# The one-hot of the first layer's expert slots: four comparisons instead of one, and its products two product groups later

## The chip, the cores and the metric

The kernel runs on one core of a Trainium2 chip. The metric is the device time of one execution in microseconds (us). TensorE is called PE here, its weight load PEld, VectorE DVE, ScalarE ACT, GpSimd POOL and SyncE SP, as in the profile.

## The reference, cut to what matters

Two layers of a network over 256 latent and 256 context tokens of width 1024. Each layer ends in a mixture of 16 experts of which every token uses two. The first layer sends all 512 tokens through it, and that is the part that the change touches:

```python
combine = jnp.sum(jax.nn.one_hot(expert_idx, N_EXPERTS, dtype=jnp.float32) * wts[..., None], axis=1)

def expert(acc, p):
    wg, wu, wd, gate_col = p
    y = (jax.nn.silu(t @ wg) * (t @ wu)) @ wd
    return acc + gate_col[:, None] * y, None
```

wg and wu are 1024 x 512, wd is 512 x 1024, all float32. The kernel does not multiply every token by every expert: for each expert it finds the tokens that chose it, gives each a slot (96 slots for an expert), gathers their rows, and multiplies only those.

## The kernel before, in words

`moe` (L1637) is called once, for the first layer, with nt = 4 tiles of 128 tokens. The second layer has functions of its own.

**Slots.** For expert e the tile `rv` holds, for each token, its rank among the tokens of that expert (0 where it did not choose it). `which` (L1678) writes the one-hot `oneh`: 128 partitions (tokens) x 4 tiles x 96 slots, 1 where the rank equals the slot's number (`iot` holds 1 to 96 in every partition). It is one DVE instruction over 384 elements, L1679. `slots_of` (L1681) multiplies the one-hot with four columns for each token (four small matmuls on PE, "products" below, into a `tr` tile of PSUM), and three small DVE instructions (L1688 to L1690) turn the sums into two index columns and a weight. `gather` (L1693) then fetches the 96 rows with an indirect DMA that POOL issues.

**The product groups.** The main loop takes the experts in order. Each expert has twelve pieces of weights: four for the gate, four for up, and four for the down product of the expert before it. They are called g0 to g3, u0 to u3 and d0 to d3 below. `gemm3` (L1751) does one piece at a time: it takes the next prepared piece, issues six matmuls of 512 columns (a product group), and calls `step`, which lets every running generator do its next bit. So whatever a generator does after its k-th `yield` is issued, on every engine, k product groups after it was begun.

**Preparing a piece.** Each piece is split into a rounded part (ACT copy, L469) and a rest (subtraction, L470), 128 x 1024 each. There are four buffers (`wb`, `wb`, `uo`, `um`), so a piece is prepared as soon as the group four before it has been multiplied. The subtraction runs on DVE for three pieces of four, and on POOL for the fourth (g3, u3, d3, all in `um`). A subtraction is called a share below.

**The generators of one expert.** `stage_a(e+3)` finds the slots and gathers: it is begun after u3 of expert e and issues the one-hot at once. After d0 it does nothing (first `yield` passed), after d1 it issues the products, after d2 the three small DVE instructions, after d3 the gather. `stage_b` (L1737) transposes gathered rows during u1 to u3. `stage_d` (L1770) issues the gating (`sg`, L1776 on DVE) after d0 and its transposes (L1781) after g1 of the next expert. `evac` scales the output rows, and `scatter` writes them back after g2.

The order on every queue is the order in which this Python program issues, and each engine takes its queue in order. The one-hots of experts 0 and 1 are made before the loop (L1826), those of experts 2 to 15 by `stage_a`, the last of them during expert 12.

Of the kernel before, what the change touches and what calls it, by code (L numbers as in the profile page):

```python
# [11 lines left out]
ALU = mybir.AluOpType  # L12
# [11 lines left out]
def bc(ap, shape):  # L24
    return ap.to_broadcast(shape)
# [64 lines left out]
def build(tc, I, out):  # L90
# [4 lines left out]
    PE, DV, SC, GP, SY = nc.tensor, nc.vector, nc.scalar, nc.gpsimd, nc.sync  # L95
# [470 lines left out]
    def quarter(u, i):  # L566

        return u[i // 4][:, 512 * (i % 4):512 * (i % 4) + 512]
# [632 lines left out]
    oh, ol = ([quarter(uo, 8 * j + c) for c in range(8)] for j in range(2))  # L1201
# [336 lines left out]
    iot = const.tile([128, 96], F32, name="iot")  # L1538
# [98 lines left out]
    def moe(l, X, streams, mem, beside, then):  # L1637
# [3 lines left out]
        nt = len(streams)  # L1641
        T = 128 * nt
        CAP = 96
# [5 lines left out]
        def mt(name, shape, bufs=1, dt=F32):  # L1649
            return mp.tile(list(shape), dt, name=name, tag=name, bufs=bufs)  # L1650
# [19 lines left out]
        def slots(rank, col):  # L1670

            oh = mt("oneh", [128, nt, CAP], dt=F32R)
            which(oh, rank)
            yield
            yield
            yield from slots_of(oh, col)

        def which(oh, rank):  # L1678
            DV.tensor_tensor(oh, bc(iot[:, None, 0:CAP], [128, nt, CAP]), bc(rank, [128, nt, CAP]), op=ALU.is_equal)  # L1679

        def slots_of(oh, col):  # L1681
            p = ps_tr()
            for t in range(nt):
                mm(p[0:CAP, 0:4], oh[:, t], col[:, t], t == 0, t == nt - 1)
            yield
            ir, ig = mt("ir", [CAP, 1], 6, I32), mt("ig", [CAP, 1], 4, I32)
            ws = mt("ws", [CAP, 1], 6)
            DV.tensor_scalar(ig, p[0:CAP, 0:1], BIG, None, op0=ALU.add)  # L1688
            DV.tensor_scalar(ir, p[0:CAP, 3:4], BIG, None, op0=ALU.add)
            DV.tensor_reduce(ws, p[0:CAP, 1:3], axis=AX.X, op=ALU.add)  # L1690
            yield ir, ig, ws
# [27 lines left out]
        def stage_a(e):  # L1719

            for r in slots(rv[:, :, 0:1, e].bitcast(F32), rv[:, :, 1:5, e]):
                if r is None:
                    yield
            ir, ig, ws = r
            IR[e] = (ir, ws)
            yield
            gather(xg[e % 2], ig)
            yield
# [38 lines left out]
        def sgt():  # L1767
            return mt("sg", [128, 512])
# [55 lines left out]
        oh = [sgt()[:, 0:nt * CAP].rearrange("p (t l) -> p t l", t=nt), mt("oneh", [128, nt, CAP], dt=F32R)]  # L1824
        for e in range(2):
            which(oh[e], rv[:, :, 0:1, e].bitcast(F32))  # L1826
# [44 lines left out]
        with tc.If(most > CAP):  # L1871
            rvD = dram.tile([128, nt * 5, 16], F32, name=f"rvD{l}")
            SY.dma_start(rvD[:, :, :], rv.bitcast(F32).rearrange("p t i e -> p (t i) e"))
            with tc.For_i(0, NEXP, 1) as e:
# [11 lines left out]
                for b in range(1, NB):  # L1886
                    DV.tensor_scalar(col[:, :, 0], col[:, :, 0], -float(CAP), None, op0=ALU.add)
                    *_, (ir, ig, ws) = slots(col[:, :, 0:1], colr)
                    gather(xg[0], ig)
                    xT = mem["ow"][2][:, 0:8 * CAP].rearrange("p (k l) -> p k l", k=8)  # L1890
# [609 lines left out]
    T, CAP = 256, 64  # L2500
# [6 lines left out]
    def pair_tile():  # L2507
        return mt("oneh", [128, 2, 2, 2, CAP], 2, F32R)
# [198 lines left out]
    with tc.If(most > CAP):  # L2707
# [3 lines left out]
        with tc.For_i(0, NEXP, 1) as e:  # L2711
# [10 lines left out]
            for b in range(1, T // CAP):  # L2722
                DV.tensor_scalar(col[:, :, 0], col[:, :, 0], -float(CAP), None, op0=ALU.add)
                oh = pair_tile()
# [68 lines left out]
```

## Time and profile before

| | us |
|---|---|
| median of 3 runs | 1588.27 (1587.4 to 1590.36) |
| the profiled execution | 1591.26 |
| its span, first to last instruction | 1589.5 |
| mean granted TensorE clock, share of full | 0.951 |
| PE busy / DVE busy / POOL busy in the span | 1397.3 / 915.4 / 617.6 |

The span is what the trace covers; the 1.76 us around it are in the time but not in the trace. The experts of the first layer run from about 650 to 965 us of the span.

### The profile page before, as it was taken

What the parts mean: (1) busy time and instruction counts of PE and PEld (TensorE: products, weight loads), DVE (VectorE), ACT (ScalarE), POOL (GpSimd) and SP (SyncE); (2) the same over time, 40 slices, a digit from 0 to 9 for tenths busy, and PEclk for the clock granted to TensorE, in tenths of its full rate; (3) what the DMA queues carried; (4) which work ended last, traced back from release to release, by engine and by line L of the source; (5) the groups of instructions that cost most, each with busy time, mean ns of one, the idle gap of its engine ahead of it and who ended that gap; (6) DMA issues with size and microseconds to landing.
All of it is one profiled execution on the core that took longest, in us unless ns stands there. A gap on an engine that the chain in (4) does not pass through costs nothing. (4 is left out here: it accounts for less than half of the span.)

```text
span 1589.5 us, 19404 instructions
## 1 busy us (share of the span) xinstructions
PE 1397.3 (88%) x7312; PEld 941.9 (59%) x7312; DVE 915.4 (58%) x1206; ACT 756.5 (48%) x1269; POOL 617.6 (39%) x398
## 2 busy tenths in 40 slices
PE   5999989877789987699999895799999888999996
PEld 2677755554466665466666673578777666444542
DVE  2665541779686466688888785635555655222223
ACT  4453435445435444477777684644444453211212
POOL 4333324877556274255555653333233223000000
PEclk8999999989899999799999998799999999999998
DMA  9266445546424153799998965422212568899994
GB/s 330 82 156 151 122 107 185 177 168 211 147 67 159 54 212 136 266 323 352 350 344 311 314 235 194 169 81 82 76 54 80 178 246 317 313 395 393 394 393 177
DMA packets 181687, 337.68 MB, mean 212 GB/s; under 512 B 7513, under 2 KB 44641, under 8 KB 181072
## 3 DMA queue, kind: packets, MB, share of 16 engines
q1 hardware_dynamic: 176112, 323.69, 59.2%
q0 software_dynamic: 4208, 8.90, 1.9%
q10 hardware_dynamic: 1264, 3.73, 0.6%
q8 instruction: 62, 1.02, 0.3%
q14 instruction: 41, 0.34, 0.1%
HBM read 329.12 MB, written 11.37 MB: 214 GB/s over the span
## 5 line engine op out<-in xcount | busy, mean ns | idle before, releaser
L470 POOL TENSOR_TENSOR wb<-wring,wb 128x1024 fp32r<-128x1024 f32 x68 | 169.6, 2497 | 276.6 <-ACT wb L469 233.6
L99 PE MATMUL acc<-hh,wb 128*128 128x512 f32 x640 | 207.4, 401 | 4.9 <-POOL wb L470 2.3
L99 PEld LDWEIGHTS acc<-hh,wb 128*128 128x128 f32 x640 | 119.7, 189 | 39.1 <-issue 5.9
L469 ACT ACTIVATE wb<-wring 128x1024 fp32r<-128x1024 f32 x88 | 92.6, 1058 | 101.8 <-PE acc L99 53.1
L99 PE MATMUL acc<-hl,wb 128*128 128x512 f32 x320 | 127.6, 399 | 0.3 <-DVE hl L595 0.2
L99 PE MATMUL acc<-wb,um 128*96 128x512 f32 (+1 forms) x480 | 120.2, 400 | 3.0 <-DVE otmp L1510 2.5
L712 DVE SCALAR_TENSOR_TENSOR ca<-u,pcol,ca 128x572 f32<-128x572 f32 x87 | 109.5, 1317 | 0.0
L99 PEld LDWEIGHTS acc<-wb,um 128*96 128x96 f32 (+1 forms) x480 | 80.4, 169 | 35.5 <-DVE otmp L1510 3.6
L2754 POOL TENSOR_TENSOR xl<-xl,fg 128x512 f32<-128x512 f32 x1 | 1.3, 1268 | 243.3 <-ACT xl L2753 243.3
L99 PE MATMUL y<-hu,hu 128*64 128x512 f32 (+2 forms) x296 | 85.4, 521 | 2.9 <-DVE hu L2137 2.8
L2586 DVE TENSOR_TENSOR sg<-sg,y 64x512 f32<-64x512 f32 x16 | 11.1, 691 | 120.6 <-ACT sg L2585 120.6
L99 PE MATMUL acc<-um,um 128*96 128x512 f32 (+2 forms) x272 | 68.1, 390 | 2.7 <-POOL um L470 2.7
L470 DVE TENSOR_TENSOR wb<-uo,wb 128x1024 fp32r<-128x1024 f32 x34 | 55.5, 1664 | 25.0 <-ACT wb L469 24.9
L99 PEld LDWEIGHTS acc<-hl,wb 128*128 128x128 f32 x320 | 60.7, 190 | 15.5 <-DVE hl L595 1.6
L470 POOL TENSOR_TENSOR um<-uo,um 128x1024 fp32r<-128x1024 f32 x19 | 48.3, 2544 | 38.9 <-ACT um L469 38.9
L99 PE MATMUL acc<-uo,um 128*96 128x512 f32 (+1 forms) x240 | 63.0, 401 | 0.0
L470 DVE TENSOR_TENSOR wb<-um,wb 128x1024 fp32r<-128x1024 f32 x30 | 51.0, 1736 | 18.3 <-ACT wb L469 18.3
L864 DVE SCALAR_TENSOR_TENSOR xa<-xin,pcol,xa 128x514 f32<-128x514 f32 x64 | 58.8, 919 | 2.3
L99 PE MATMUL acc<-wring,sT 128*32 128x512 f32 x336 | 47.9, 651 | 10.7 <-DMA wring<-in_mod_w_dram 7.6
L2585 ACT ACTIVATE sg<-y 64x512 f32<-64x512 f32 x16 | 9.5, 591 | 96.9 <-PE y L99 96.9
L99 PEld LDWEIGHTS y<-hu,hu 128*64 128x64 f32 (+2 forms) x296 | 31.8, 151 | 38.1 <-issue 33.7
L99 PEld LDWEIGHTS acc<-um,um 128*96 128x96 f32 (+1 forms) x272 | 43.5, 174 | 17.9 <-POOL um L470 3.8
(661 smaller groups left out, 3479.0 us busy)
## 6 DMA issues: line engine op xcount, KB each, us to landing
wring<-in_mod_w_dram SPq DMA_DIRECT2D x42, 1024.0 KB, 5.3
wring<-in_moe_w_gate_dram SPq DMA_DIRECT2D x18, 1024.0 KB, 7.5
uo<-in_moe_w_up_dram SPq DMA_DIRECT2D x17, 1024.0 KB, 8.1
hu<-in_moe_w_gate_dram SPq DMA_DIRECT2D x16, 1024.0 KB, 14.6
wring<-in_moe_w_down_dram SPq DMA_DIRECT2D x14, 1024.0 KB, 7.5
uo<-in_moe_w_down_dram SPq DMA_DIRECT2D x13, 1024.0 KB, 7.4
um<-in_moe_w_up_dram SPq DMA_DIRECT2D x13, 1024.0 KB, 8.0
wring<-in_hg_w_in_dram SPq DMA_DIRECT2D x13, 1024.0 KB, 5.1
```

The costliest lines, as they stand in the source:

```text
L99: PE.matmul(o, l, r, start=start, stop=stop, skip_group_check=True)
L469: SC.activation(hv, w, AF.Copy)
L470: eng.tensor_tensor(lv, w, hv.bitcast(F32), op=ALU.subtract)
L712: DV.scalar_tensor_tensor(a, x, w, a, op0=ALU.mult, op1=ALU.add)
L864: DV.scalar_tensor_tensor(a[:, 0:514], x[:, k:k + 514], par("sc_w", 16 * k + i), a[:, 0:514], op0=ALU.mult, op1=ALU.add)
L2585: SC.activation(s_[up], acc[0:CAP], AF.Silu)
L2586: DV.tensor_tensor(s_[up], s_[up], acc[up], op=ALU.mult)
L2754: GP.tensor_tensor(o, o, fg[hf], op=ALU.mult)
```

## The change

`which` writes the one-hot in four instructions, one for each tile of 128 tokens: 96 slot numbers are compared with one value per partition (that token's rank), instead of two tensors of 384 elements with each other. It concerns all 16 experts. And `slots`, from which `stage_a` takes its steps, yields four times instead of twice between the one-hot and the products. The products are thus issued after d3 instead of after d1, the three small DVE instructions after g0 of the next expert instead of after d2, and the gather after g1 instead of after d3. (The loop for experts with more than 96 tokens also calls `slots`, but takes all its steps at once.)

```diff
             oh = mt("oneh", [128, nt, CAP], dt=F32R)
             which(oh, rank)
-            yield
-            yield
+            for _ in range(4):
+                yield
             yield from slots_of(oh, col)
 
         def which(oh, rank):
-            DV.tensor_tensor(oh, bc(iot[:, None, 0:CAP], [128, nt, CAP]), bc(rank, [128, nt, CAP]), op=ALU.is_equal)
+            for t in range(nt):
+                DV.tensor_scalar(oh[:, t], iot[:, 0:CAP], rank[:, t], None, op0=ALU.is_equal)
```

## Rows read from the trace of the kernel before

**Rows 1.** The page: the chain that ended last, share of the span by engine.

```profile
PE 28%; DVE 5%; issue 2%; ACT 2%; POOL 1%; DMA 0%; POOLq 0%; DVEq 0%; ACTq 0%; SPq 0%
```

**Rows 2.** Waits of PE, 648 to 925 us (us in total, times, longest).

```profile
PE tr L99 <- DVE oneh L1679: 17.7, 11, 2.2
```

**Rows 3.** The tile `oneh`: its DVE instruction (duration ns min/median/max).

```profile
L1679 DVE TENSOR_TENSOR oneh<-iot,sm x15: 542/2273/2481, 642.1 to 904.2; 128x384 fp32r<-128x384 f32 x15
```

**Rows 4.** Timeline of one expert (start us, us, what; idle before in brackets).

```profile
759.05 2.94 PE L99 MATMUL y<-wb,um 128*96 128x512 f32 x12
...
760.45 2.43 POOL L470 TENSOR_TENSOR um<-uo,um 128x1024 fp32r<-128x1024 f32 x1 [3.64 <-ACT um L469]
...
761.02 2.27 DVE L1679 TENSOR_TENSOR oneh<-iot,sm 128x384 fp32r<-128x384 f32 x1
...
763.22 0.67 DVE L1776 TENSOR_TENSOR sg<-sg,acc 96x512 f32<-96x512 f32 x1
...
763.44 0.47 PE L99 MATMUL tr<-sm,oneh 128*96 128x4 f32 x4 [1.45 <-DVE oneh L1679]
...
763.78 1.61 PE L99 MATMUL y<-uo,um 128*96 128x512 f32 x6
763.82 2.34 DVE L470 TENSOR_TENSOR wb<-rows_g,wb 128x1024 fp32r<-128x1024 f32 x2
...
765.23 1.55 PE L99 MATMUL y<-um,um 128*96 128x512 f32 x6
...
766.50 0.97 POOL L1694 DMA_INDIRECT um<-hD,ig  x1 [3.62 <-DVE ws L1690]
766.52 1.24 DVE L470 TENSOR_TENSOR uo<-rows_s,uo 128x1024 fp32r<-128x1024 f32 x1 [0.16 <-ACT uo L469]
766.62 2.94 PE L99 MATMUL acc<-wb,um 128*96 128x512 f32 x12
766.88 1.06 ACT L469 ACTIVATE um<-rows_s 128x1024 fp32r<-128x1024 f32 x1 [0.39 <-PE y L99]
...
768.03 2.41 POOL L470 TENSOR_TENSOR um<-rows_s,um 128x1024 fp32r<-128x1024 f32 x1 [0.56 <-ACT um L469]
...
769.67 1.61 PE L99 MATMUL acc<-uo,um 128*96 128x512 f32 x6
...
778.73 2.95 PE L99 MATMUL y<-wb,ah 128*96 128x512 f32 x12
```

**Rows 5.** Timeline, later experts, where no one-hot is left: g0 of two of them.

```profile
930.70 2.94 PE L99 MATMUL acc<-wb,um 128*96 128x512 f32 x12
...
948.36 2.94 PE L99 MATMUL acc<-wb,um 128*96 128x512 f32 x12
```

**Rows 6.** Stretches: us, PE PEld DVE ACT POOL busy (count), PEclk, DMA share, GB/s.

```profile
704.09:802.60 98.51, 91.21 (x440) 64.08 (x440) 84.28 (x86) 75.95 (x90) 50.92 (x25) 1.00 1.00 349
...
1390.00:1410.00 20.00, 20.00 (x100) 7.69 (x100) 3.17 (x5) 2.84 (x5) 0.00 (x0) 1.00 1.05 393
```

**Rows 7.** Source lines of comparisons and products with one value per partition.

```profile
L2613 DVE TENSOR_SCALAR back<-masks,tw x16: 345/354/356, 1375.2 to 1573.4; 128x256 fp32r<-128x256 f32 x16
...
L582 DVE TENSOR_SCALAR xld<-xld,rst x4: 753/753/754, 8.6 to 13.0; 128x1024 f32<-128x1024 f32 x4
```

**Rows 8.** Timeline: instructions with values per partition, beside POOL and in a row.

```profile
83.47 2.38 POOL L470 TENSOR_TENSOR wb<-wring,wb 128x1024 fp32r<-128x1024 f32 x1 [3.56 <-ACT wb L469]
83.97 2.17 DVE L862 TENSOR_SCALAR xa<-xin,pcol 128x514 f32<-128x514 f32 x1 [0.80 <-ACT xin L858]
...
284.91 0.64 DVE L708 TENSOR_SCALAR ca<-u,pcol 128x572 f32<-128x572 f32 x1
285.46 1.29 DVE L710 TENSOR_SCALAR ca<-u,pcol 128x572 f32<-128x572 f32 x1
```

**Rows 9.** Timeline: a run of five DVE instructions, and POOL asking within it.

```profile
329.17 7.01 DVE L712 SCALAR_TENSOR_TENSOR ca<-u,pcol,ca 128x572 f32<-128x572 f32 x5
330.35 1.55 POOL L1081 TENSOR_TENSOR sb1h<-mL,lah 128x512 fp32r<-128x512 f32 x1
```

## The prediction

> **What bounds the kernel now.** I read the chain that ended last first: PE has by far the largest part of it, 28% of the span against 5% for DVE, and DMA has none [rows 1]. So what the experts' stage saves on PE reaches the end. In that stage PE waits for hardly anything but the one-hot: 11 waits, 17.7 us [rows 2]. That is the most the change can take away, 1.1% of the time.
>
> The one-hot is late because of its neighbour, not its size. Alone it takes 0.54 us, its median is 2.27 [rows 3]. In the timeline of one expert [rows 4] it is issued at 761.02, while POOL is busy with the share of d3 from 760.45 to 762.88, and ends at 763.29, 0.41 us after POOL. An instruction of DVE with two inputs in SBUF stands still while POOL's subtraction runs, and does its elements then. PE has finished d1 long before and starts the products at 763.44.
>
> Without that wait the expert's twelve groups take 19.70 - 1.45 = 18.25 us (778.73 - 759.05, rounded, less the wait). The last experts, which have no one-hot and no products, show that such a pace is possible: 948.36 - 930.70 = 17.66 us [rows 5].
>
> **The change, step by step.** Times below are offsets from the start of d0, 759.05 in [rows 4].
>
> *The four comparisons.* Two rows with one value per partition give the slope: 753 - 354 ns for 768 more elements, 0.52 ns each [rows 7]. So 96 elements take 354 - 160 x 0.52 = 271 ns. In a row the next one starts 0.09 us before the one ahead ends (284.91 + 0.64 against 285.46 [rows 8]), so each further one adds 0.18. Alone: 0.27 + 3 x 0.18 = 0.81 us against 0.54.
>
> Does POOL stop them too? An instruction of this kind, issued at 83.97 with POOL busy until 85.85, ended at 86.14 [rows 8]: it was stopped, and ended 0.29 after, which is its 514 elements at 0.52 ns. I take that, so the first comparison ends 0.07 after POOL and the other three 0.54 later: +3.83 + 0.61 = +4.44, 0.20 later than now (+4.24). The bounds: not stopped at all, they end at +1.97 + 0.81 = +2.78; stopped and without any overlap, at +4.71. The stop by POOL agrees with the Trainium skill, "SBUF — State Buffer", section "SBUF: two separate sides": the port pair is an exclusive lock, and the one that starts first keeps it for its whole instruction. Before the loop the same price adds about 0.3 us to experts 0 and 1, where DVE is what PE waits for next; it is counted.
>
> *The products.* After d3 they no longer wait. A group takes 1.39 us (765.23 to 766.62), so d0 to d3 end at +5.56, and the one-hot has been ready since +4.44. The products take 0.34 (763.44 to 763.78) and end at +5.90. Here the 1.45 is gone: the work that hides the one-hot is d2 and d3, and it hides 2 x 1.39 us.
>
> *What is late next.* DVE's queue behind the one-hot holds the gating and the shares of g0, g1 and g2, and the one-hot has only become longer. Now the share of g0 starts 0.53 after the one-hot's end (763.82), and two shares take 2.34. With four comparisons g0's share ends at +4.97 + 1.17 = +6.14, g1's at +7.31. PE needs g0's at +5.90 and gets it at +6.29, with the 0.15 from DVE's end to PE's start that the products show: a new wait of 0.39. From g0 to g2 takes 3.05 (766.62 to 769.67), so g2 is due at +9.34, against +10.62 before.
>
> The share of g2 stands third in DVE's queue and can start at +7.24. In the kernel before, it starts at 766.52, and POOL's share of g3 only at 768.03: no conflict. POOL's share follows PE: from d3's start to ACT's copy is 1.65, from there to POOL 1.15. PE is now earlier, d3 starts at +4.17, and POOL asks at +6.97, inside g1's share and 0.27 before DVE gets to g2's. Does POOL get in between two DVE instructions that follow each other? At 330.35 a POOL instruction asks within a run of five that lasts until 336.18, and it is through at 331.90 [rows 9]: yes.
>
> If POOL is first (a long period), its share runs from +7.31 for 2.41 to +9.72. DVE's share of g2 takes 1.24 alone, less the 0.13 of start-up that a stopped instruction has behind it (0.54 against 0.41), and ends at +10.83. PE starts g2 at +10.98, where it was +10.62: **0.36 longer than now**. If DVE is first (a short period), g2's share is done at +8.4, g2 starts in time, POOL's share ends at +10.8, g3 waits some 0.18, and the period is 1.28 - 0.18 = **1.10 shorter**.
>
> Which of the two comes is decided by 0.27 us, and each prepares the other: after a long one PE has rested at g2 and DVE has caught up before the next d2, so POOL's share of d3 ends a little earlier; after a short one PE has run ahead and DVE's shares come late. I take them in turn, -0.37 on the mean.
>
> *The gather and the small ones.* The three small DVE instructions move behind g2's share, and the gather (0.97 on POOL) from ahead of g3's share to behind it. Its rows are needed by transposes more than a whole period later. If that cover were gone, each would cost at most its length. Nothing moves on SP's queue; the order in which the PSUM tiles are taken stays the same.
>
> **Sum.** 11 x -0.37 = -4.1, and +0.3 at the start: -3.8. The profiled execution took 1591.26 (span 1589.5 and 1.76 around it), 2.99 above the median of the runs, 1588.27. On the median: about 1584.4.
>
> **The rivals.**
>
> 1. *POOL is first every time.* It decides as soon as DVE reaches g2's share later than +6.97; by my walk that is so at the start (+7.24). For it: the margin has the right sign. Against it: a long period lets DVE catch up. Price: 11 x 0.36 + 0.3 = +4.3, 1592.5, slower.
> 2. *DVE is first every time*, because the comparisons are quicker than I think or POOL is handed over later. 11 x -1.10 + 0.3 = -11.8: 1576.5.
> 3. *The comparisons aren't stopped by POOL.* They end at +2.78, DVE is ahead of every share, PE waits for nothing: -17.7 + 0.3, 1570.9. The row at 83.97 speaks against it, though its instruction has two values per partition and more elements.
> 4. *The comparisons don't overlap.* They end at +4.71, 0.27 later, every period is long and by 0.63: +7.2, 1595.5. The rows that follow each other with 0.09 of overlap speak against it. The Trainium skill, "VectorE: DVE Perf Modes", section "The DRAIN you can't avoid", speaks for it: the next instruction starts only when the pipe is empty, and one should keep the number of instructions low. By that rule this change goes the wrong way. I give it 0.05.
> 5. *DMA becomes the bound.* 349 GB/s over 19.70 us are 6.88 MB for each expert [rows 6]; at the 393 of the last stage that is 17.5 us, below the 18.25 without any wait. So it stops nothing.
>
> **How the numbers follow.** Forecast 0.48, rival 1 0.26, rival 2 0.15, rival 3 0.06, rival 4 0.05. About 0.2%, 3.2 us, is what a measurement of this kernel can tell from no change. The forecast lies at the edge of that: of its 0.48 I count 0.32 as faster, 0.15 as the same and 0.01 as slower. Rival 1 gives 0.11 to the same and 0.15 to slower, rivals 2 and 3 are faster, rival 4 is slower. Faster 0.53, same 0.26, slower 0.21. The range leaves out rivals 3 and 4 and some of the edges of the others: 1575 to 1593; the forecast's own is 1580 to 1588.
>
> **What would show it.** In the trace after, the wait of PE for the one-hot is gone. In its place stand waits for a share of DVE: about 0.4 us ahead of g0 and, in every other expert, 1.6 us ahead of g2, where DVE's share of `uo` takes over 3 us behind POOL's share of `um`. The first comparison should last some 2 us, the other three under 0.3 each. Periods of about 18.6 and 20.1 us should follow in turn. If the comparisons last 0.3 us while POOL runs, rival 3 is right; if all periods are 20 us, rival 1; if the comparisons start 0.27 apart, rival 4. If the periods shrink to 18.25 with the comparisons stopped, my order on the port is wrong.

## The result, and the profile after

The changed kernel takes 1575.76 us (median of six runs), beside 1589.32 for the kernel before in six runs on the same chip: 13.6 us less. The ratio of the means is 0.9897, with a 95% interval from 0.9868 to 0.9926, which is 11.8 to 21.0 us less. One of the six runs, with 2002.81 us at a granted clock of 0.646, where the others have 0.948 to 0.955, counts in that median and not in the ratio. The forecast was 3.9 us less; the measured time lies just inside the low end of the range, near rival 2.

The page after, the span, the engines and the chain that ended last [rows 1]:

```profile
span 1567.9 us, 19455 instructions
...
PE 1391.5 (89%) x7312; PEld 937.4 (60%) x7312; DVE 933.8 (60%) x1254; ACT 755.0 (48%) x1269; POOL 638.1 (41%) x398
...
PE 28%; DVE 5%; issue 2%; ACT 2%; POOL 1%; DMA 0%; POOLq 0%; DVEq 0%; ACTq 0%; SPq 0%
```

The shares of the chain are the same to the per cent. A gain of 1% is not seen there; it is seen in the waits of PE, in the same stretch as [rows 2] (us in total, times, longest):

```profile
PE acc L99 <- DVE wb L470: 2.9, 8, 0.4
PE acc L99 <- POOL um L470: 2.8, 1, 2.8
PE tr L1747 <- DVE um L1736: 2.4, 1, 2.4
PE y L99 <- POOL um L470: 0.5, 2, 0.3
```

The 17.7 us for the one-hot are gone. In their place stand eight waits of 0.4 for the share of g0. The profiled execution took 1569.71 us, 21.6 less than the profiled one of before, but 8.4 of that lie ahead of d0 of expert 1, the first d0 of the loop, and behind d0 of expert 14: 5.0 (680.99 against 675.94) and 3.4, mostly in code that is the same in both. Between these two starts lie thirteen periods. Here they are for both kernels, each the difference of two starts of d0 in the timeline:

```
before 18.15 20.45 19.72 19.74 19.68 19.72 19.71 19.69 21.24 23.74 18.56 23.74 17.68   sum 261.82
after  18.90 18.19 19.06 19.05 19.05 19.03 19.05 19.03 19.03 22.28 18.57 19.74 17.68   sum 248.66
```

13.2 us less, near the 13.6 of the medians and inside the interval of the ratio. It has three parts: six regular experts at -0.66 (-4.0), the first two periods (-1.5), and three that were longer before, 21.24, 23.74 and 23.74, with their counterparts after (-7.7). Long and short ones don't take turns: the regular period is 19.05 each time.

One regular expert after, in the timeline, to be laid beside [rows 4] (start us, us, what; idle before in brackets). d0 starts at 751.14:

```profile
751.14 2.94 PE L99 MATMUL y<-wb,um 128*96 128x512 f32 x12
...
752.30 1.21 DVE L470 TENSOR_TENSOR uo<-uo,uo 128x1024 fp32r<-128x1024 f32 x1
...
752.54 3.25 POOL L470 TENSOR_TENSOR um<-uo,um 128x1024 fp32r<-128x1024 f32 x1 [2.84 <-ACT um L469]
...
753.44 0.54 DVE L1736 TENSOR_TENSOR um<-tr,um 128x384 fp32r<-128x384 f32 x1
...
753.90 2.49 DVE L1680 TENSOR_SCALAR oneh<-iot,sm 128x96 fp32r<-128x96 f32 x4
753.92 1.56 PE L99 MATMUL y<-uo,um 128*96 128x512 f32 x6
...
755.32 1.92 PE L99 MATMUL y<-um,um 128*96 128x512 f32 x6
...
756.91 2.35 DVE L470 TENSOR_TENSOR wb<-rows_g,wb 128x1024 fp32r<-128x1024 f32 x2
757.08 0.42 PE L99 MATMUL tr<-sm,oneh 128*96 128x4 f32 x4
...
758.18 2.78 PE L99 MATMUL acc<-wb,um 128*96 128x512 f32 x11 [0.37 <-DVE wb L470]
...
758.47 4.22 POOL L470 TENSOR_TENSOR um<-rows_s,um 128x1024 fp32r<-128x1024 f32 x1 [2.68 <-ACT um L469]
759.18 1.21 DVE L470 TENSOR_TENSOR uo<-rows_s,uo 128x1024 fp32r<-128x1024 f32 x1
...
761.07 1.61 PE L99 MATMUL acc<-uo,um 128*96 128x512 f32 x6
...
762.52 1.63 PE L99 MATMUL acc<-um,um 128*96 128x512 f32 x6
...
770.19 2.94 PE L99 MATMUL y<-wb,ah 128*96 128x512 f32 x12
```

Read it from the one-hot down. The four comparisons are still held up: they start at 753.90 and end at 756.39, 0.60 after POOL's share of d3 (752.54 + 3.25 = 755.79). But PE is busy with d2 and d3 meanwhile, and the products start at 757.08 without a wait. Then the two lines that decide: POOL asks for g3's share at 758.47, DVE starts g2's share only at 759.18, and still DVE goes first. It takes its usual 1.21, ends at 760.39, and POOL's share ends 2.30 after that, at 762.69, where a share of POOL takes 2.41 alone. g2 starts without a wait at 761.07.

What sets 19.05? The pace without waits is 18.25. The wait ahead of the second matmul of g0 adds 0.37. d3 takes 1.92, where it took 1.55 [rows 4]: 0.37 for POOL's share of d3, which asks at +1.40 as before but has to wait for DVE's share at 752.30. g3 loses 0.08 in the same way. Together 19.07. Behind these waits is one queue, DVE's. The same expert, from d0 to d0 (us; PE, PEld, DVE, ACT, POOL busy; clock; DMA share; GB/s, as in [rows 6]):

```profile
751.14:770.19 19.05, 18.56 (x89) 12.74 (x88) 18.77 (x21) 15.26 (x18) 13.06 (x5) 1.00 1.04 358
```

DVE is occupied for 18.77 of 19.05 us, the time it stands still for POOL included. The kernel is not bound by what DVE computes, but DVE has no slack left.

**The irregular periods** changed by other amounts, for two reasons. One is the wait itself. In three of them PE had waited 2.24, 1.51 and 2.22 us before the products, in the timeline of before:

```profile
704.32 0.47 PE L99 MATMUL tr<-sm,oneh 128*96 128x4 f32 x4 [2.24 <-DVE oneh L1679]
...
863.54 0.47 PE L99 MATMUL tr<-sm,oneh 128*96 128x4 f32 x4 [1.51 <-DVE oneh L1679]
...
906.56 0.47 PE L99 MATMUL tr<-sm,oneh 128*96 128x4 f32 x4 [2.22 <-DVE oneh L1679]
```

and their periods shrank by 2.26, 1.46 and 4.00. In the first the whole wait came back; the other two need the second reason, the clock. Stretches of d2 and d3 in three experts of the kernel before, the third one regular, and one behind a later wait (columns as in [rows 6]):

```profile
842.60:847.00 4.40, 4.40 (x14) 2.92 (x14) 3.37 (x7) 1.06 (x1) 0.97 (x1) 0.61 0.97 351
906.90:911.60 4.70, 4.70 (x17) 3.18 (x17) 3.81 (x7) 1.06 (x1) 0.97 (x1) 0.64 1.05 363
763.78:768.00 4.22, 4.22 (x20) 2.96 (x20) 3.83 (x7) 2.18 (x3) 0.97 (x1) 1.00 1.01 364
880.60:884.00 3.40, 3.40 (x8) 2.32 (x9) 1.96 (x3) 0.87 (x1) 3.40 (x10) 0.50 0.64 187
```

In the first two the granted clock falls to a mean of 0.61 and 0.64, so for most of the stretch to the lower level of 1.2 GHz. From the first matmul of d2 to the end of d3 it takes 4.40 us in the first (842.61 to 847.01), 2.84 in the regular one (763.78 to 766.62). That is 1.56 more, and 21.24 is 1.54 above 19.70. In the second it is 4.34 (906.89 to 911.23), 1.50 more; with the wait of 2.22 that is 3.72 of the 4.00. PE had waited for the one-hot right ahead of both stretches, 1.49 and 2.22 us.

The last stretch belongs to the period with the wait of 1.51. There PE also waits for POOL's share, in both kernels alike; before, the clock falls behind that wait, and after it doesn't (first line before, second after):

```profile
880.59 2.45 PE L99 MATMUL acc<-um,um 128*96 128x512 f32 x5 [2.75 <-POOL um L470]
867.37 1.40 PE L99 MATMUL acc<-um,um 128*96 128x512 f32 x5 [2.83 <-POOL um L470]
```

From there to the next d0 it is 2.24 us before (882.83 - 880.59) and 1.24 after (868.61 - 867.37). So 1.00 of this period's 1.46 is the clock, and no more than 0.46 of the wait came back, since a wait of 0.38 for g0's share stands in this period after the change. The first period went the other way, 0.75 longer, and that is the clock again: after the change it is at 0.50 from 674.5 to 677.9, and d0 and d1 take 3.68 us (675.94 to 679.62) instead of 2.79 (680.99 to 683.78). So the clock's part in the 13.2 us is about 3.2: 1.56, 1.50 and 1.00 gained, 0.89 lost. After that start, the whole stretch of the experts is at full clock (both lines of the kernel after):

```profile
674.50:677.90 3.40, 3.40 (x10) 2.24 (x9) 1.82 (x7) 1.62 (x3) 0.52 (x1) 0.50 1.03 297
684.00:950.00 266.00, 258.31 (x1236) 179.66 (x1235) 251.83 (x259) 214.98 (x256) 175.99 (x89) 1.00 0.93 327
```

### The profile page after: what moved, and what is told of

The parts are those of the page before. It is cut to its first block, busy times and chain, and to the rows that moved or that the text cites. A ratio compares the mean times of both kernels' runs of the same rounds, so it can differ in the third digit from the quotient of the medians.

```text
span 1567.9 us, 19455 instructions
## 1 busy us (share of the span) xinstructions
PE 1391.5 (89%) x7312; PEld 937.4 (60%) x7312; DVE 933.8 (60%) x1254; ACT 755.0 (48%) x1269; POOL 638.1 (41%) x398
## 5 line engine op out<-in xcount | busy, mean ns | idle before, releaser
L99 PE MATMUL acc<-wb,um 128*96 128x512 f32 (+1 forms) x480 | 123.5, 404 | 5.8 <-DVE wb L470 2.9
L470 POOL TENSOR_TENSOR um<-wring,um 128x1024 fp32r<-128x1024 f32 x16 | 51.4, 3215 | 51.9 <-ACT um L469 49.7
L470 DVE TENSOR_TENSOR wb<-uo,wb 128x1024 fp32r<-128x1024 f32 x34 | 60.8, 1822 | 11.7 <-ACT wb L469 11.2
L470 POOL TENSOR_TENSOR um<-uo,um 128x1024 fp32r<-128x1024 f32 x19 | 53.5, 2818 | 31.5 <-ACT um L469 31.4
L470 DVE TENSOR_TENSOR wb<-um,wb 128x1024 fp32r<-128x1024 f32 x30 | 57.6, 1956 | 5.2 <-ACT wb L469 4.5
L99 PEld LDWEIGHTS acc<-um,um 128*96 128x96 f32 (+1 forms) x272 | 43.1, 175 | 18.8 <-POOL um L470 5.8
```

The lines of the kernel that those rows point to most:

```text
L99: PE.matmul(o, l, r, start=start, stop=stop, skip_group_check=True)
L470: eng.tensor_tensor(lv, w, hv.bitcast(F32), op=ALU.subtract)
```

## The experiments

"Theory A" in the quoted texts: the later products carry the gain, PE's wait goes behind d2 and d3, and the period is set by DVE's queue, where POOL gets no turn between shares that follow each other. The rivals are put in each text.

**The changed kernel again**, as the yardstick.

> The changed kernel once more, as the yardstick of this call. Both theories: the time is about 0.990 of the kernel before, an expert's period is 19.05 us, and the periods do not alternate.

1574.33 us, ratio 0.9908 (0.988 to 0.9935); regular period 19.02 to 19.07. The result stands, and the second kind of period that the forecast had taking turns with the first is absent here too.

**One half alone: only the delay.** The one-hot is one comparison as before, its products two groups later.

```diff
-            for t in range(nt):
-                DV.tensor_scalar(oh[:, t], iot[:, 0:CAP], rank[:, t], None, op0=ALU.is_equal)
+            DV.tensor_tensor(oh, bc(iot[:, None, 0:CAP], [128, nt, CAP]), bc(rank, [128, nt, CAP]), op=ALU.is_equal)
```

> One comparison as before, but the products four steps after it. Theory A (the delay takes PE's wait away, and what is then the bound is DVE's queue with its stops at the port): DVE is relieved of the 0.2 us by which four comparisons end later, so the period is about 18.85 us and the time some 2 us below that of the changed kernel. Rival B (the four comparisons have a part in the gain, since they leave the port between them): the period is longer than 19.05, and the gain is mostly gone.

1573.26 us, ratio 0.9896 (0.9872 to 0.992), period 18.82 to 18.88. The delay alone carries the whole gain. The four comparisons cost 0.2 us in each regular period, the 0.20 of the prediction's first step.

**The other half alone: four comparisons, no delay.**

```diff
-            for _ in range(4):
+            for _ in range(2):
```

> Four comparisons, but the products two steps after them as before. Theory A: PE waits for the one-hot 0.2 us longer than in the kernel before, some 1.65 us in each expert, the period is 19.9 us, and the time is 1 to 3 us above the kernel before. Rival B: part of the gain is there, the wait is well below 1.45 us.

1595.88 us, ratio 1.004 (1.0025 to 1.0055): slower, as theory A has it, but by some 6 us where it has 1 to 3. PE waits for the one-hot as long in total as before [rows 2], and in the first half of the experts the clock falls in every other one (waits of PE: us in total, times, longest; then stretches):

```profile
PE tr L99 <- DVE oneh L1680: 17.5, 12, 1.9
```

```profile
700.00:720.00 20.00, 18.11 (x81) 12.61 (x80) 15.91 (x20) 13.41 (x17) 10.07 (x5) 0.91 0.96 332
720.00:740.00 20.00, 18.87 (x92) 13.30 (x91) 18.05 (x21) 15.72 (x19) 11.72 (x5) 1.00 0.97 339
740.00:760.00 20.00, 18.20 (x82) 12.68 (x81) 15.89 (x20) 13.81 (x17) 10.80 (x5) 0.91 0.93 324
760.00:780.00 20.00, 18.90 (x91) 13.29 (x90) 18.03 (x21) 15.72 (x20) 11.67 (x5) 1.00 0.98 339
```

The periods there go 21.86, 19.55, 21.83, 19.55, 21.64, 19.59; then come 20.23 and 20.17 without a fall. Waits of 1.89 and 1.80 stand ahead of the slow stretches above, waits of 1.13 and 1.10 ahead of the others. Of the 2.28 between a long and a short period (21.83 - 19.55), 0.76 is the longer wait (1.89 - 1.13); the other 1.52 are the clock, about the 1.56 and 1.50 of the kernel before. So a wait costs its length, and where the clock falls behind it, about 1.5 us more.

**Half of the delay**, with the single comparison: `range(3)` instead of `range(4)`.

> One comparison, the products three steps after it, so after d2. One group of 1.39 us lies over the wait of 1.45. Theory A: DVE's queue is the bound as in the kernel with four steps, so the period is about 18.9 us and the time within 2 us of that kernel. Rival B: each group hides only its own length, and what is left of the wait, and the shares behind it, put the period between 19.05 and 19.7.

1572.32 us, ratio 0.9901 (0.9875 to 0.9928), period 18.8 to 18.95. Eight waits for the one-hot of at most 0.7 remain, and the time is the same: one group later already does it. That fits a pace that DVE's queue sets: what PE waits for in one place it doesn't wait for in the next.

**Who gets the port?** The prediction had POOL come in between two DVE instructions that follow each other. One small DVE instruction that reads only PSUM (96 values) is put between the shares of g1 and g2; its result is used by nothing.

```diff
-            for _ in range(5 if e < NEXP - 1 else 1):
+            for k in range(5 if e < NEXP - 1 else 1):
+                if k == 2:
+                    DV.tensor_scalar(mt("gap", [CAP, 1], 2), au[0:CAP, 0:1], 1.0, None, op0=ALU.mult)
                 yield
```

> The changed kernel with one more small DVE instruction, 96 x 1 from PSUM (0.15 us, read by nobody), between DVE's share of g1 and its share of g2. Theory A (the port stays with DVE as long as its instructions with two inputs in SBUF follow each other, and POOL gets in only where DVE does something else between): POOL's share of g3, which asks while g1's share runs, now goes first, DVE's share of g2 stands 2.3 us behind it, PE waits over 1 us ahead of g2, periods of 20 us or more come back, and the time is 8 to 18 us above the changed kernel. Rival B (POOL is late for another reason, the order of the two does not hang on the gap): the period grows by 0.1 us at most, the time by 1 us.

1576.54 us, ratio 0.9922 (0.9896 to 0.9947), period 19.08 to 19.14. That is what rival B expects, not theory A, and the timeline shows more:

```profile
760.24 4.27 POOL L470 TENSOR_TENSOR um<-rows_s,um 128x1024 fp32r<-128x1024 f32 x1 [2.69 <-ACT um L469]
...
760.95 0.14 DVE L1780 TENSOR_SCALAR gap<-acc 96x1 f32<-96x1 f32 x1
761.02 1.21 DVE L470 TENSOR_TENSOR uo<-rows_s,uo 128x1024 fp32r<-128x1024 f32 x1
```

The small instruction starts 0.07 before g1's share ends (761.03), and g2's share starts 0.07 after that. There is no pause at all, so this run doesn't decide whether one would matter. The same was tried with three and with six of them (the edit is shown against the run with one):

```diff
-                    DV.tensor_scalar(mt("gap", [CAP, 1], 2), au[0:CAP, 0:1], 1.0, None, op0=ALU.mult)
+                    for _ in range(3):
+                        DV.tensor_scalar(mt("gap", [CAP, 1], 6), au[0:CAP, 0:1], 1.0, None, op0=ALU.mult)
```

> The changed kernel with three small instructions of DVE (96 values out of PSUM each, the one so far was followed by the share of g2 0.07 us after it began) between the shares of g1 and g2. They leave POOL's share of g3, which has been asking since well before, about 0.2 us in which DVE reads nothing from SBUF. Theory A2 (POOL gets in wherever DVE leaves SBUF alone for longer than a hand-over takes, and 0.07 was too short): POOL's share of g3 goes first in most experts, DVE's share of g2 takes over 3 us and ends some 2.3 us later, PE waits over 1 us ahead of g2, the period is 20 us or more, and the time lies 8 to 18 us above the changed kernel. Rival (POOL comes only when DVE's queue holds no further instruction that wants SBUF, however short the pause is): g2's share still goes first, the period grows by the 0.2 us in DVE's queue at most, 19.05 to 19.3 us, 0 to 3 us in all.

> As the run with three, with six small instructions, some 0.4 to 0.5 us in which DVE reads nothing from SBUF; that is nearly the 0.54 us of the split out of PSUM behind which POOL did get in. Theory A2: POOL's share of g3 goes first in every expert, the share of g2 ends some 2.3 us later, the period is 20 us or more, 8 to 18 us above the changed kernel. Rival (POOL waits for an empty queue): g2's share goes first, the period is longer by 0.45 us at most, up to 19.5 us, and the time up to 6 us above the changed kernel. If three do not let POOL in and six do, the hand-over takes between 0.2 and 0.45 us.

Three: 1585.83 us, ratio 0.9977 (0.9962 to 0.9992), period 20.22 to 20.29. Six: 1583.17, 0.9966 (0.9946 to 0.9986), 20.21 to 20.31. What theory A2 forecast came already with three. The timeline of one expert with three:

```profile
760.50 2.34 DVE L470 TENSOR_TENSOR wb<-rows_g,wb 128x1024 fp32r<-128x1024 f32 x2
...
762.06 3.08 POOL L470 TENSOR_TENSOR um<-rows_s,um 128x1024 fp32r<-128x1024 f32 x1 [2.68 <-ACT um L469]
762.77 0.27 DVE L1781 TENSOR_SCALAR gap<-acc 96x1 f32<-96x1 f32 x3
762.97 3.25 DVE L470 TENSOR_TENSOR uo<-rows_s,uo 128x1024 fp32r<-128x1024 f32 x1
...
766.28 1.40 PE L99 MATMUL acc<-uo,um 128*96 128x512 f32 x5 [1.15 <-DVE uo L470]
```

g1's share ends at 762.84 and g2's is issued at 762.97. In those 0.13 us POOL comes in; g2's share takes 3.25 instead of 1.21, PE waits 1.15 inside g2, and the period grows by 1.2 us, six times the small instructions' own 0.2. This is the forecast's long period, 20.25 where it had 20.06. The kernel with six leaves 0.32 us and gives the same period: beyond 0.13 the length of the pause doesn't matter.

But a pause isn't what decides for all instructions of DVE. The trace of before can be asked, in its earlier stages. First the run of [rows 9] one instruction at a time, then two products of 512 elements without a value per partition, and POOL's share that asks during the first:

```profile
329.17 1.82 DVE L712 SCALAR_TENSOR_TENSOR ca<-u,pcol,ca 128x572 f32<-128x572 f32 x1
330.92 1.58 DVE L712 SCALAR_TENSOR_TENSOR ca<-u,pcol,ca 128x572 f32<-128x572 f32 x1
...
559.93 0.68 DVE L1439 TENSOR_TENSOR um<-um,uo 128x512 f32<-128x512 f32 x1
560.25 2.58 POOL L470 TENSOR_TENSOR wb<-wring,wb 128x1024 fp32r<-128x1024 f32 x1 [1.40 <-ACT wb L469]
560.53 2.85 DVE L1439 TENSOR_TENSOR um<-um,uo 128x512 f32<-128x512 f32 x1
```

In both, the second instruction is issued 0.07 or 0.08 before the first ends (330.99, 560.61), just as between two shares, and yet POOL goes first: it is through at 331.90 and at 562.83, and the second instruction of DVE ends 0.60 and 0.55 after it. Why POOL gets in there and not between two shares stays open.

**How full is DVE's queue?** Each of the four comparisons is done twice (`for t in 2 * list(range(nt))`); the second writes the same values.

> The changed kernel with each of the four comparisons done twice, the second time over the same result: 0.72 us more of DVE for each expert. Theory A (after the change DVE's queue with its stops is the bound): the period grows by 0.72 to 19.8 us, and the time by 8 to 9 us above the changed kernel. Rival B (PE is the bound, the comparisons lie under d2 and d3): the period grows by less than 0.3 us and the time by less than 3.

1586.83 us, ratio 0.9988 (0.9976 to 1.0), period 19.73 to 19.79, so +0.71: the 4 x 0.18 of four more comparisons, almost exactly, and PE's wait for g0's share grows from 0.4 to 1.1. What is added to DVE's queue now costs its whole length. (Theory A's 8 to 9 us came less exactly: the thirteen periods together grew by 7.0 us, the time by some 12. The difference lies outside these periods, and its cause is open.)

**A better place.** If what hurts is a one-hot standing behind POOL's share of d3 in DVE's queue, it belongs ahead of it: the slots are begun after u2, one group earlier, and the products keep their place behind d3 with one more `yield`.

```diff
+            if j == 2 and e + 3 < NEXP:
+                begin(stage_a(e + 3))
...
-            for _ in range(4):
+            for _ in range(5):
```

> The changed kernel with the slots begun one group earlier, after u2, and five steps before the products, so that these stay after d3. Theory A (DVE's stop at the port during the comparisons is what it loses): the comparisons run ahead of POOL's share of d3, in 0.8 us instead of 2.5, the split and the gating, which need no port, lie under POOL's share, the period falls towards PE's own 18.25, to 18.3 to 18.6 us, and the time by 5 to 8 us below the changed kernel. Rival B (the stop only moves on to the share of g0): the period stays within 0.2 us of 19.05.

> As the kernel before in this call, begun after u2 with five steps, but with the one comparison of the kernel before. Theory A: DVE has 0.2 to 0.3 us less to do, the period is at PE's own, 18.2 to 18.4 us, and the time is 0 to 3 us below that of the four comparisons begun early. Rival B: within 0.2 us of 18.85, as with the products alone moved.

With four comparisons 1571.55 us, ratio 0.989 (0.9871 to 0.9909), period 18.47 to 18.54; with the single comparison **1566.53 us, ratio 0.9872 (0.985 to 0.9894)**, regular periods 18.1 to 18.3, the lowest time of all. The comparisons are no longer stopped (timeline of the first of the two, then of the second):

```profile
754.17 0.79 DVE L1680 TENSOR_SCALAR oneh<-iot,sm 128x96 fp32r<-128x96 f32 x4
```

```profile
752.49 0.54 DVE L1679 TENSOR_TENSOR oneh<-iot,sm 128x384 fp32r<-128x384 f32 x1
```

and in the second kernel PE works through two experts without a gap, while DVE has slack again (a stretch, columns as above):

```profile
751.00:790.00 39.00, 38.96 (x188) 27.31 (x187) 35.91 (x38) 32.63 (x40) 23.18 (x11) 1.00 1.04 375
```

The intervals of the later ratios overlap with that of the changed kernel, so the order among the faster kernels rests on the periods more than on the times. By its ratio, the first of the two gains only 1 to 3 us on the changed kernel, where theory A has 5 to 8; its thirteen periods together are 4.6 us shorter.

## Why the prediction was wrong, and where it was right

- **The cover by d2 and d3**: right. The products moved behind d3, wait for nothing, and the 1.45 is gone.
- **The comparisons**: right. Four of them take 0.79 to 0.80 alone (0.81 forecast), they are stopped by POOL and end 0.60 after it (0.61). So rivals 3 and 4 are out. By the Trainium skill, "VectorE: DVE Perf Modes", section "The DRAIN you can't avoid", the next one starts only when the pipe is empty, but the section adds that an instruction which is not held starts earlier, and rival 4 left that out. Here each further comparison costs 0.18 us, where one takes some 0.26 alone, and the measurement decides.
- **The new wait at g0**: right, 0.37 (0.39 forecast).
- **"Does POOL get in between two DVE instructions that follow each other? ... yes."** This is the step that failed. POOL asked 0.7 us ahead of DVE in every regular expert, and DVE's share went first; the 0.27 us by which the forecast decided between long and short decide nothing. So the regular period became 0.66 shorter each time, where the forecast took 0.36 longer and 1.10 shorter in turn, -0.37 on the mean. The reading of [rows 9] was right for its five instructions and didn't carry over to the shares. Between two shares POOL gets in with a pause of 0.13 us and not without one; the instructions of [rows 9] leave no pause either, so what tells them from the shares is not known.
- So **rival 2's order** came, every time, at rival 2's time: 1576.5 against 1575.76. Its sum is right by two errors, though. Its period was 18.6 and 19.05 came, because POOL's share of d3 now has to wait for DVE and d3 takes 0.37 longer, a wait that the prediction did not have (it left POOL's end at +3.83; it came at +4.65). That cost is made up for by gains in the irregular periods.
- These gains were in none of the cases, and this is the second step that failed: **the prediction took one regular expert for all of them**, in the sum 11 x -0.37 = -4.1. The six regular periods gave -4.0; the other seven gave -9.2. The wait of 2.24 came back whole, and the clock, which had no term in the sum, gave about 3.2: falls of 1.56, 1.50 and 1.00 us behind waits of PE were gone, and one of 0.89 came in the first period. Nor were the 17.7 us of [rows 2] "the most the change can take away": a wait can cost more than its length.
- **The +0.3 at the start** had the wrong sign. From the routing's first instruction (L1607) to the first of the three small ones it took 3.69 us before (640.10 to 643.79) and 3.41 after (635.37 to 638.78), because the first products now start 0.42 us after the comparisons begin (636.91 to 637.33), not 0.70 (641.64 to 642.34): 0.42 is one comparison and the 0.15 from DVE to PE, so they wait only for the first of the four.
- **DMA** bounds nothing up to 375 GB/s and a period of 18.25, in the last of the runs: rival 5 was rightly left out.

## What to carry to other kernels

Count where an engine's queue is full, not only where it works: an instruction that is stopped by a neighbour's operation blocks everything behind it, and moving its consumer helps only until that queue is the bound. It is better to issue the stopped instruction before its neighbour begins. And a gain should be summed over all the periods of a stage, not over a clean one times their number: the irregular ones held more than half of it here, 9.2 of 13.2 us. And a row that shows who goes first holds for the instructions in it; for others it is a guess.

## What the runs showed of the hardware that was not expected

- Between DVE's shares it matters not who asks first but whether DVE pauses. POOL stood in line from 758.47 while DVE's next share, issued at 759.18, went first; 0.13 us between two shares of DVE let POOL in, and cost 1.2 us for each expert. Small instructions that look harmless between two large ones can thus cost six times their length. It is no rule for every pair of DVE instructions: at 560.25 POOL got in between two of 512 elements without a pause.
- The granted clock fell to 1.2 GHz behind waits of PE of 1.49 to 2.75 us, but not behind each, and the length of the wait doesn't tell which: at 906.56 after 2.22 it did, at 704.32 after 2.24 it stayed at 1.00 (704.66 to 708.90). At 842.28 after 1.49 it did, at 822.60 after 1.49 it did not. Behind the wait for POOL's share it fell before the change (2.75) and not after (2.83). What tells these cases apart stays open.
